# Quarter-size first loads, idle transposes, rstd from x^T and new planner figures in a transformer trunk kernel

## The chip, the cores and the metric

The kernel runs on one core of a Trainium2 chip. The metric is the device time of one execution in microseconds. Three runs of the kernel before gave 1015.75, 1016.25 and 1017.58 us; the median, 1016.25 us, is the time to beat. The engines are named as the profile names them: PE (TensorE matmul), PEld (its weight loads), DVE (VectorE), ACT (ScalarE), POOL (GpSimd) and SP, whose queue issues every DMA here.

## What is computed

A decoder trunk of two layers over 256 tokens of width 1024, all in float32. Each layer is FFN, mixer, FFN; layer 0 mixes by stick-breaking attention beside a convolution, layer 1 by gated linear attention (GLA). Every block is wrapped in norms:

```
def rms_norm(x, g):
    y = x * lax.rsqrt(jnp.mean(x * x, axis=-1, keepdims=True) + 1e-6)
    return y * g

h = x
for l in range(2):
    h = h + 0.5 * rms_norm(swiglu(rms_norm(h, g[0]), ffn1_in, ffn1_out), g[1])
    m = even_mixer(rms_norm(h, g[2])) if l == 0 else odd_mixer(rms_norm(h, g[2]))
    h = h + rms_norm(m, g[3])
    h = h + 0.5 * rms_norm(swiglu(rms_norm(h, g[4]), ffn2_in, ffn2_out), g[5])
```

Six phases follow each other, p = 0 to 5. The change rewrites the very start of phase 0: the norm of x that stands ahead of the first FFN.

## The kernel before

**Weights and products.** A weight block is 128x1024 float32, 512 KB. SP loads it into a ring of four `raw` buffers. ACT casts it to a rounded high part `hi` (L310), DVE subtracts that from the raw block to get the low part `lo` (L311), and both go into rings of nine. PE then makes each product three times, high by high, high by low and low by high (`mm3`, L334, L335, L336). So a block costs one DMA, one ACT cast, one DVE subtraction and a run of matmuls, and the buffers come free in that order.

**The planner.** The class `Plan` writes the order of every engine's instructions before the kernel is built. Each step is added with an estimated cost; a list scheduler then picks, among the steps that are ready, the one that comes first in the program. It adds `LATENCY` (80 ns) to each hand-over between engines, 1700 ns ahead of a DMA and 900 ns behind one, and takes a DMA to cost its bytes over 360. An engine keeps the order so written: whatever stands first on it and waits holds what stands behind it.

**The start (class `Entry`).** Phase 0 doesn't wait for the norm. The kernel also gets x transposed (`x_t`, two halves of 512 KB, L388) and the first gain (`g_first`, L390). ACT scales and rounds x^T by the gain (`xgh`, L395), DVE takes the rest (`xgl`, L397), and the first two groups of products `pt` (`proj_entry`, 48 matmuls of 512 columns each) run on these without rstd. Meanwhile x itself is loaded in four pieces (`h`, L300), ACT squares it with a running sum (L344), DVE adds epsilon (L349), and POOL raises the sum to the power -1/2 (`rstd_of`, L340). The gates of the first FFN (`ut`, L578 on ACT, L580 on DVE) apply rstd to the products. `scaled` then spreads rstd over a PSUM bank by two products (`rstd_rows`, L427), DVE multiplies x^T by it (L432, eight times), and ACT and DVE split that into `xT` (L442, L443), which all later products of this FFN (`pw`, L534 and L535) need.

**Later places that the prediction speaks of.** In each FFN the first four gates stand on PE banks that the later `pw` products take over: `pw` of the third pair waits until DVE has read the last gate `ut_11` (L584) from its bank. In GLA, PE makes the low-rank gate product `gz` (L937) from a small tile that DVE copies out of PSUM (`gla_small`, L932), amid the weight splits `lo_gq` (L311). The transposes of normed rows (`xtr_p`, L479) wait for DVE's `xn_p` (L467).

Of the kernel before, what the change touches and what calls it, by code (L numbers as in the profile page):

```python
# [9 lines left out]
F32 = mybir.dt.float32  # L10
# [26 lines left out]
OUT_TAIL = 8  # L37
CONV_PE = 6
# [29 lines left out]
class Plan:  # L68
# [3 lines left out]
    LATENCY = 80  # L72
    DMA_START, DMA_DONE = 1700, 900
# [60 lines left out]
    def dma(self, nbytes, fn, r, w):  # L134
        return self.add("dma", nbytes / 360.0, fn, r, w)
# [77 lines left out]
def trunk(ctx: ExitStack, tc: tile.TileContext, x, x_t, g_first, norm_g, ffn_in, ffn_out, hyb_in, hyb_out,  # L213
# [83 lines left out]
    def load_x(t):  # L297
        for n in range(2):
            s = slice(n * H, (n + 1) * H)
            dma(P * H * 4, lambda t=t, s=s: nc.sync.dma_start(h[t][:, s], x[t * P:(t + 1) * P, s]),  # L300
                [], [(h[t], n)])

    def load_gain(i):
        g = buf("gain", [P, D], F32, f"gain{i}")
        dma(P * D * 4, lambda: nc.sync.dma_start(g[:, :], norm_g[i].partition_broadcast(P)), [], [g])
# [7 lines left out]
    def weights(src, name, slots=None, first=False):  # L313

        res = []
        for i in range(src.shape[0]):
            raw = buf("raw", [P, D], F32, f"raw_{name}_{i}")
            dma(P * D * 4, lambda i=i, raw=raw: nc.sync.dma_start(raw[:, :], src[i]), [], [raw])
# [4 lines left out]
            if first and not i:  # L323
                for n in range(2):
                    s = slice(n * H, (n + 1) * H)
                    split(H, lambda hi=hi, s=s: hi[:, s], lambda lo=lo, s=s: lo[:, s], lambda raw=raw, s=s: raw[:, s], [raw], [(hi, n), (lo, n)])
# [12 lines left out]
    def rstd_of(st):  # L339
        gps(470, lambda: nc.gpsimd.tensor_tensor(st[:, 3:4], st[:, 2:3], mhalf[:, :], op=ALU.pow),  # L340
# [31 lines left out]
    class Entry:  # L372
# [14 lines left out]
        def load(self, b):  # L387
            dma(P * D * 4, lambda: nc.sync.dma_start(self.raw[b][:, :], x_t[b]), [], [self.raw[b]])  # L388
            if b == 0:
                dma(P * KT * 4, lambda: nc.sync.dma_start(self.gk[:, :], g_first), [], [self.gk])  # L390

        def split(self, b):
            raw, (hi, lo) = self.raw[b], (self.parts[q][b] for q in range(2))
            for k in range(4 * b, 4 * b + 4):
                act(S, lambda k=k: nc.scalar.activation(self.cols(hi, k), self.cols(raw, k), AF.Copy, scale=self.g(k)),  # L395
                    [raw, self.gk], [(hi, k)], ptrs=1)
                dve(S, lambda k=k: nc.vector.scalar_tensor_tensor(  # L397
                    self.cols(lo, k), self.cols(raw, k), self.g(k), self.cols(hi, k).bitcast(F32),
                    op0=ALU.mult, op1=ALU.subtract), [raw, self.gk, (hi, k)], [(lo, k)], ptr=True)
# [6 lines left out]

        def statistics(self):
            for t in range(NT):
                load_x(t)
            for t in range(NT):  # L410
                y, st = buf("y", [P, D], F32, f"xsq_p0{t}"), self.st[t]
                for n in range(2):
                    sum_squares(y, n * H, st, n, lambda t=t, n=n: h[t][:, n * H:(n + 1) * H], 1.0 / 32.0,
                                [(h[t], n)], False)
                add_eps(st, EPS)
                rstd_of(st)

        def scaled(self, xT):

            small = slot(6, "entry_small")  # L420
# [777 lines left out]
```

## Time and profile before

| what | us |
|---|---|
| median of three runs | 1016.25 |
| the profiled execution | 1020.89 |
| its span, first to last instruction | 1019.2 |
| PE busy in it | 1000.6 (98%) |
| DVE busy | 679.0 (67%) |
| ACT busy | 568.4 (56%) |
| DMA engines' mean share | about half |

The profiled execution is 4.64 us longer than the median; differences worked out from its trace are applied to the median. Times in rows are microseconds from the start of the span unless marked ns. A group of like instructions is shown in one row with a count, so the duration of such a row is that of the whole group. Matmul durations overlap: one that "took" 0.39 us may have the next behind it after 0.23 us, and spacing is then read from start to start.

### The profile page before, as it was taken

Reading aid. Unit: us, or ns where it says so; the run is one execution under the profiler, and the core shown is the slowest. Engines: PE = TensorE matmul, PEld = TensorE weight load, DVE = VectorE, ACT = ScalarE, POOL = GpSimd, SP = SyncE. Lnnn points to the kernel's source line nnn. Section 1 sums busy time; section 2 is a strip of 40 time slices with the busy share of each in tenths; the row PEclk is TensorE's granted clock in tenths of the full one; section 3 lists DMA queues with packets and bytes.
Section 4 is the critical chain, followed back from the end, with each engine's and each line's share of the span. In section 5 each row is a group of like instructions: output and inputs, shape, how many; then the busy total and the mean of one; then the engine's idle time right before and its main releaser. Section 6 shows DMA issues by size and latency. Waiting matters only on the chain.

```text
span 1019.2 us, 13982 instructions
## 1 busy us (share of the span) xinstructions
PE 1000.6 (98%) x5216; PEld 845.2 (83%) x5216; DVE 679.0 (67%) x1103; ACT 568.4 (56%) x979; POOL 57.2 (6%) x109
## 2 busy tenths in 40 slices
PE   6999999999999999999999999999999999999997
PEld 5888888888777888888888888888889888888885
DVE  4875658669868766668666666774568586656662
ACT  6764657585556654557455545654464375545551
POOL 2730000100001000000000000000000110000000
PEclk9999999999999999999999999999989999999999
DMA  8676557552034746567446465772641156555531
GB/s 320 220 251 200 180 195 257 197 174 76 21 125 165 266 162 213 166 207 237 162 171 211 161 215 164 231 246 84 211 166 64 42 182 231 182 190 187 199 110 42
DMA packets 50342, 180.46 MB, mean 177 GB/s; under 512 B 5713, under 2 KB 5969, under 8 KB 50274
## 3 DMA queue, kind: packets, MB, share of 16 engines
q1 hardware_dynamic: 50274, 179.57, 52.1%
q8 instruction: 41, 0.67, 0.3%
q14 instruction: 27, 0.22, 0.1%
HBM read 178.50 MB, written 1.05 MB: 176 GB/s over the span
## 4 chain that ended last, share of the span: by engine, by line
PE 92%; DVE 3%; DMA 2%; ACT 1%; issue 1%; POOL 1%; SPq 0%; DVEq 0%; POOLq 0%; ACTq 0%
PE pw L534 26%; PE pw L535 13%; PE o_f L334 8%; PE o_f L335 8%; PE o_f L336 8%; PE pt L335 2%; PE pt L334 2%; PE pt L336 2%; DMA raw_fi<-ffn_in 2%; PE gv L335 1%; PE gv L334 1%; PE gv L336 1%; PE cv L832 1%; PE sp L1027 1%; PE xtr_p L479 1%; PE hq L334 1%
## 5 line engine op out<-in xcount | busy, mean ns | idle before, releaser
L534 PE MATMUL pw<-xT_p,hi_fi 128*128 128x512 f32 x1152 | 409.8, 399 | 1.4 <-DVE ut L584 1.4
L535 PE MATMUL pw<-xT_p,lo_fi 128*128 128x256 f32 x1152 | 323.4, 281 | 0.0
L534 PEld LDWEIGHTS pw<-xT_p,hi_fi 128*128 128x128 f32 x1152 | 216.6, 188 | 55.4 <-issue 1.3
L311 DVE TENSOR_TENSOR lo_fi<-raw_fi,hi_fi 128x1024 fp32r<-128x1024 f32 (+1 forms) x177 | 212.7, 1216 | 50.8 <-ACT hi_fi L310 50.4
L535 PEld LDWEIGHTS pw<-xT_p,lo_fi 128*128 128x128 f32 x1152 | 217.8, 189 | 2.2
L310 ACT CAST hi_fi<-raw_fi 128x1024 fp32r<-128x1024 f32 (+1 forms) x177 | 181.2, 1045 | 42.7 <-DMA raw_fi<-ffn_in 22.7
L658 DVE TENSOR_TENSOR uab<-pw,uab 128x256 f32<-128x256 f32 x144 | 60.5, 421 | 114.3 <-ACT uab L657 114.3
L657 ACT COPY uab<-pw 128x256 f32<-128x256 f32 x144 | 53.6, 372 | 135.3 <-PE pw L535 135.0
L334 PE MATMUL o_f<-hi_fo,uTh 128*128 128x512 f32 x224 | 88.2, 394 | 0.0
L335 PE MATMUL o_f<-lo_fo,uTh 128*128 128x512 f32 x224 | 87.9, 392 | 0.0
L336 PE MATMUL o_f<-hi_fo,uTl 128*128 128x512 f32 x224 | 87.2, 389 | 0.0
L311 DVE TENSOR_TENSOR lo_fo<-raw_fo,hi_fo 128x1024 fp32r<-128x1024 f32 x56 | 68.3, 1222 | 13.4 <-ACT hi_fo L310 12.6
L310 ACT CAST hi_fo<-raw_fo 128x1024 fp32r<-128x1024 f32 x56 | 58.8, 1049 | 5.6 <-DMA raw_fo<-ffn_out 2.2
L340 POOL TENSOR_TENSOR pst_p<-pst_p,mhalf 128x1 f32<-128x1 f32 x12 | 8.2, 685 | 790.2 <-DVE pst_p L349 775.5
L334 PE MATMUL o_f<-h_fo,uTh 128*128 128x512 f32 x128 | 50.8, 397 | 0.0
L336 PE MATMUL o_f<-h_fo,uTl 128*128 128x512 f32 x128 | 50.5, 395 | 0.0
L335 PE MATMUL o_f<-l_fo,uTh 128*128 128x512 f32 x128 | 50.5, 394 | 0.0
L334 PEld LDWEIGHTS o_f<-hi_fo,uTh 128*128 128x128 f32 x224 | 42.1, 188 | 9.7
L336 PEld LDWEIGHTS o_f<-hi_fo,uTl 128*128 128x128 f32 x224 | 42.1, 188 | 9.2
L556 ACT CAST uTh<-uw 128x256 fp32r<-128x256 f32 x72 | 29.3, 407 | 35.7 <-DVE uw L660 35.5
L335 PEld LDWEIGHTS o_f<-lo_fo,uTh 128*128 128x128 f32 x224 | 42.1, 188 | 6.7
L659 ACT ACTIVATE uw<-uab 128x256 f32<-128x256 f32 x72 | 30.1, 418 | 31.1 <-DVE uab L658 31.1
(249 smaller groups left out, 1674.1 us busy)
## 6 DMA issues: line engine op xcount, KB each, us to landing
raw_fi<-ffn_in SPq DMA_DIRECT2D x176, 512.0 KB, 4.5
raw_fo<-ffn_out SPq DMA_DIRECT2D x88, 512.0 KB, 4.2
raw_gv<-gla_in SPq DMA_DIRECT2D x16, 512.0 KB, 4.5
gain<-norm_g SPq DMA_DIRECT2D x11, 512.0 KB, 4.6
raw_hu<-hyb_in SPq DMA_DIRECT2D x8, 512.0 KB, 4.7
raw_hq<-hyb_in SPq DMA_DIRECT2D x8, 512.0 KB, 4.1
raw_ho<-hyb_out SPq DMA_DIRECT2D x8, 512.0 KB, 4.3
raw_gq<-gla_in SPq DMA_DIRECT2D x8, 512.0 KB, 5.1
```

The source lines that it names most:

```text
L310: act(n, lambda: nc.scalar.copy(hi(), src()), r, [w[0]], psum=psum)
L311: dve(n, lambda: nc.vector.tensor_sub(lo(), src(), hi().bitcast(F32)), list(r) + [w[0]], [w[1]])
L334: nc.tensor.matmul(ps, lhsT=lhs[0], rhs=rhs[0], start=start, stop=False)
L335: nc.tensor.matmul(ps, lhsT=lhs[0], rhs=rhs[1], start=False, stop=False)
L336: nc.tensor.matmul(ps, lhsT=lhs[1], rhs=rhs[0], start=False, stop=stop)
L479: nc.tensor.transpose(ps[:, k * P:(k + 1) * P], y[:, c * P:(c + 1) * P], ident[:, :])
L534: nc.tensor.matmul(pss[i][:, :], lhsT=hi, rhs=xT[:, k, :, :], start=k == 0, stop=False)
L535: nc.tensor.matmul(pss[i][:, S:], lhsT=lo, rhs=xT[:, k, 0, :], start=False, stop=k == KT - 1)
L556: act(n, lambda: nc.scalar.copy(h_[:, s], src()), r, [(h_, 0), (h_, 1)], psum=psum)
L657: act(S, lambda v=v, ps=ps: nc.scalar.copy(v(), ps[:, S:]), [ps], [(g, i)], psum=True)
L658: dve(S, lambda v=v, ps=ps: nc.vector.tensor_add(v(), ps[:, :S], v()), [ps, (g, i)], [(g, i)])
L659: act(S, lambda u=u, g=g: nc.scalar.activation(u[:, :], g[:, :S], AF.Silu), [(g, 0)], [u], table=SILU)
```

## The change

Phase 0 begins in another way. PE first runs 24 transposes of the identity into a bank that nobody reads (`Entry.warm`). x^T comes in four loads of 256 KB, and the first weight block in two; the casts and scalings follow these pieces. The sum of squares is taken from x^T: ACT squares it without a running sum (two instructions of 128x1024), PE makes 16 products of a 128x128 block of squares by one column of ones (`entry_sums`, each product 128x1), DVE adds epsilon from that bank, POOL raises to the power as before. `scaled` comes ahead of the gates in the program. x itself and the first two gains, 2 MB in all, are loaded only halfway through the first FFN. The planner's figures change as well: `LATENCY` 150, 600 ns behind a DMA, bytes over 285, 690 ns for the power. These set the order of the whole program, so instructions move in all phases.

```diff
+WARM = 24
-    LATENCY = 80
-    DMA_START, DMA_DONE = 1700, 900
+    LATENCY = 150
+    DMA_START, DMA_DONE = 1700, 600
-    def dma(self, nbytes, fn, r, w):
-        return self.add("dma", nbytes / 360.0, fn, r, w)
+    def dma(self, nbytes, fn, r, w, after=()):
+        return self.add("dma", nbytes / 285.0, fn, r, w, after=after)
...
-        gps(470, lambda: nc.gpsimd.tensor_tensor(st[:, 3:4], st[:, 2:3], mhalf[:, :], op=ALU.pow),
+        gps(690, lambda: nc.gpsimd.tensor_tensor(st[:, 3:4], st[:, 2:3], mhalf[:, :], op=ALU.pow),
...
+        def load(self, i):
+            raw, s = self.raw[i // 2], slice(i % 2 * H, (i % 2 + 1) * H)
+            dma(P * H * 4, lambda: nc.sync.dma_start(raw[:, s], x_t[i // 2, :, s]), [], [(raw, 2 * i), (raw, 2 * i + 1)])
...
+        def warm(self):
+            ps = buf("out", [P, H], F32, "warm")
+            def run():
+                for _ in range(WARM):
+                    nc.tensor.transpose(ps[:, :P], ident[:, :], ident[:, :])
+            pe(WARM * 4 * P, run, [ident], [ps])
...
         def statistics(self):
+            small = self.small = slot(6, "entry_small")
+            fill((small, "1"), lambda: small[:, :P], 1.0)
+            sq = [buf("y", [P, D], F32, f"xsq_p0{b}") for b in range(2)]
+            for b in range(2):
+                act(D, lambda b=b: nc.scalar.activation(sq[b][:, :], self.raw[b][:, :], AF.Square, scale=1.0 / 32.0),
+                    [self.raw[b]], [sq[b]])
+            ps = bank("tr", "entry_sums")
+            def sums():
+                for t in range(NT):
+                    for k in range(KT):
+                        nc.tensor.matmul(ps[:, t:t + 1], lhsT=self.cols(sq[k // 4], k)[:, t * P:(t + 1) * P],
+                                         rhs=small[:, :1], start=k == 0, stop=k == KT - 1)
+            pe(2 * KT * 200, sums, [*sq, (small, "1")], [ps])
             for t in range(NT):
-                load_x(t)
...
+                dve(1, lambda t=t, st=st: nc.vector.tensor_scalar_add(st[:, 2:3], ps[:, t:t + 1], EPS), [ps], [st])
                 rstd_of(st)
...
+                        w = blocks(0, 1, True)
                         entry.load(1)
                         entry.split(1)
+                        w += blocks(1, 1)
+                        for i in (2, 3):
+                            entry.load(i)
+                            entry.split(i)
+                        entry.statistics()
...
+            if entry and j == NJ // 2:
+                entry.late = [plan.ops[-1]]
...
+                late = () if p else entry.late
+                if not p:
+                    for i in range(NT):
+                        load_x(i, late)
+                nxt["post"] = load_gain(layer * 6 + part * 2 + 1, late)
```

At the start ACT's order was this (`hi_fi_00_0` and `hi_fi_00_1` are the first two weight blocks, `x_t_180` and `x_t_209` the halves of x^T):

```order
L395 ACTIVATE xgh_195<-x_t_180,g_first 128x256 x4
L310 CAST hi_fi_00_0_206<-raw_fi_00_0_193 128x512 x2
L310 CAST hi_fi_00_1_219<-raw_fi_00_1_198 128x1024
L395 ACTIVATE xgh_232<-x_t_209,g_first 128x256 x4
L310 CAST hi_fi_01_0_249<-raw_fi_01_0_221 128x1024
L310 CAST hi_fi_01_1_262<-raw_fi_01_1_235 128x1024
```

It is now this (`hi_fi_t_0_226` and `hi_fi_t_0_248` are the first two weight blocks):

```order
L403 ACTIVATE xgh_220<-x_t_180,g_first 128x256 x2
L311 CAST hi_fi_t_0_226<-raw_fi_t_0_218 128x512 x2
L403 ACTIVATE xgh_220<-x_t_180,g_first 128x256 x2
L430 ACTIVATE xsq_p_239<-x_t_180 128x1024
L311 CAST hi_fi_t_0_248<-raw_fi_t_0_233 128x1024
L403 ACTIVATE xgh_258<-x_t_242,g_first 128x256 x4
L430 ACTIVATE xsq_p_276<-x_t_242 128x1024
L311 CAST hi_fi_t_0_285<-raw_fi_t_0_260 128x1024
L311 CAST hi_fi_t_1_311<-raw_fi_t_1_278 128x1024
```

The two squares now stand ahead of the casts of the second and of the third weight block. On PE, 18 matmuls of the first group of products stand between the transposes and the sums; the end of these and what follows reads now:

```order
L340 MATMUL pt_10_250<-hi_fi_t_0_248,xgh_220 128x512
L341 MATMUL pt_10_250<-lo_fi_t_0_262,xgh_220 128x512
L342 MATMUL pt_10_250<-hi_fi_t_0_248,xgl_224 128x512
L437 MATMUL entry_sums<-entry_small,xsq_p_239 128x1 x4
L437 MATMUL entry_sums<-entry_small,xsq_p_276 128x1 x4
```

The two rows of sums come once more for the second 128 tokens; the other 30 matmuls of the group stand behind them, and behind those the two `rstd_rows` products, where before they stood in the midst of the second group.

In the last FFN (and alike in the two before it) ACT's order around the last gate `ut_11` was this:

```order
L310 CAST hi_fi_6_0_8081<-raw_fi_6_0_8055 128x1024
L310 CAST hi_fi_6_1_8093<-raw_fi_6_1_8071 128x1024
L310 CAST uTh_0_7993<-ptr_10_8095 128x128
L583 ACTIVATE ut_11_8112<-pt_11_8041 128x256
L310 CAST hi_fo_2_0_8114<-raw_fo_2_0_8089 128x1024
```

It is now:

```order
L311 CAST hi_fi_6_0_8130<-raw_fi_6_0_8108 128x1024
L608 ACTIVATE ut_11_8139<-pt_11_8084 128x256
L311 CAST uTh_0_8034<-ptr_10_8132 128x128
L311 CAST hi_fi_6_1_8151<-raw_fi_6_1_8120 128x1024
L311 CAST uTh_1_8041<-ptr_10_8132 128x128
```

The gate and the small cast moved ahead of a weight cast that waits for a load; on DVE the second half of the gate moved ahead of that block's subtraction too.

In GLA, DVE's order around the copy of `gla_small` was this:

```order
L311 TENSOR_TENSOR lo_gq_0_6960<-raw_gq_0_6916,hi_gq_0_6932 128x1024
L918 TENSOR_TENSOR rg_6893<-rg_6893,gla_small 128x512
L311 TENSOR_TENSOR lo_gq_1_6969<-raw_gq_1_6928,hi_gq_1_6964 128x1024
L932 COPY gla_small<-glr 16x256
L311 TENSOR_TENSOR lo_gout_0_6991<-raw_gout_0_6962,hi_gout_0_6984 128x1024
```

It is now:

```order
L952 TENSOR_TENSOR rg_6936<-rg_6936,gla_small 128x512
L312 TENSOR_TENSOR lo_gq_0_7006<-raw_gq_0_6959,hi_gq_0_7001 128x1024
L966 COPY gla_small<-glr 16x256
L312 TENSOR_TENSOR lo_gq_1_7026<-raw_gq_1_6997,hi_gq_1_7008 128x1024
L312 TENSOR_TENSOR lo_gout_0_7038<-raw_gout_0_7004,hi_gout_0_7030 128x1024
```

The copy moved one weight split forward; PE's order there is the same: eight steps of `glr`, four of `gq`, then `gz`.

## Rows read from the trace of the kernel before

**Rows 1.** The page: busy time, share of the span, instructions of each engine.

```profile
PE 1000.6 (98%) x5216; PEld 845.2 (83%) x5216; DVE 679.0 (67%) x1103; ACT 568.4 (56%) x979; POOL 57.2 (6%) x109
```

**Rows 2.** PE's waits: line, releaser, us in total, times, longest.

```profile
PE pt L334 <- ACT hi_fi L310: 8.4, 1, 8.4
PE pw L534 <- DVE ut L584: 1.4, 2, 1.0
PE gz L937 <- DVE gla_small L932: 0.9, 1, 0.9
PE xtr_p L479 <- DVE xn_p L467: 0.5, 2, 0.3
```

**Rows 3.** The chain that ended last, its start: start, us, what.

```profile
1.73 5.98 DMA raw_fi<-ffn_in
7.73 0.63 ACT hi_fi L310
```

**Rows 4.** Windows: length, busy (instructions) of PE, PEld, DVE, ACT, POOL; clock, DMA, GB/s.

```profile
8.40:14.20 5.80, 5.80 (x13) 4.30 (x14) 5.37 (x9) 5.30 (x9) 0.00 (x0) 1.00 0.98 354
14.20:20.00 5.80, 5.80 (x26) 4.70 (x26) 3.60 (x4) 4.02 (x9) 0.51 (x1) 1.00 0.98 341
```

**Rows 5.** DMA issues, the one at 2.67 us: count, KB, us to landing.

```profile
x_t<-x_t SPq DMA_DIRECT2D x1, 512.0 KB, 7.6
```

**Rows 6.** ACT and DVE at the start: start, us, instruction [idle before].

```profile
4.67 1.70 ACT L395 ACTIVATE xgh<-x_t,g_first 128x256 fp32r<-128x256 f32 x4 [2.59 <-DMA g_first<-g_first]
...
16.84 1.05 ACT L310 CAST hi_fi<-raw_fi 128x1024 fp32r<-128x1024 f32 x1 [1.78 <-DMA raw_fi<-ffn_in]
17.79 0.63 ACT L344 ACTIVATE xsq_p<-h 128x512 f32<-128x512 f32 x1
...
24.54 3.22 DVE L432 SCALAR_TENSOR_TENSOR x_t<-x_t,g_first,rstd_rows 128x256 f32<-128x256 f32 x8 [0.79 <-PE rstd_rows L427]
```

**Rows 7.** PE from 21.2 us on: start, us, instruction [idle before].

```profile
22.27 0.39 PE L336 MATMUL pt<-hi_fi,xgl 128*128 128x512 f32 x1
...
23.89 0.61 PE L427 MATMUL rstd_rows<-entry_small 128*128 128x128 f32 x4
24.25 0.48 PE L334 MATMUL pt<-hi_fi,xgh 128*128 128x512 f32 x1
...
32.35 0.50 PE L335 MATMUL pt<-lo_fi,xgh 128*128 128x512 f32 x1 [0.21 <-DVE lo_fi L311]
...
35.02 0.39 PE L534 MATMUL pw<-xT_p,hi_fi 128*128 128x512 f32 x1
```

**Rows 8.** GLA, DVE and PE at 741 to 745 us, same columns.

```profile
741.65 1.22 DVE L311 TENSOR_TENSOR lo_gq<-raw_gq,hi_gq 128x1024 fp32r<-128x1024 f32 x1
...
742.10 0.28 PE L336 MATMUL gq<-xT_p,lo_gq 128*128 128x256 f32 x1
742.78 0.40 DVE L932 COPY gla_small<-glr 16x256 f32<-16x256 f32 x1
...
743.24 2.34 PE L937 MATMUL gz<-gla_small 17*128 17x512 f32 x4 [0.86 <-DVE gla_small L932]
```

**Rows 9.** Windows behind that place, and one of 40 us, columns as in rows 4.

```profile
744.00:746.00 2.00, 2.00 (x5) 0.67 (x4) 0.32 (x1) 1.58 (x2) 0.00 (x0) 0.68 0.96 383
746.00:748.00 2.00, 2.00 (x11) 2.00 (x11) 0.03 (x1) 1.99 (x5) 0.00 (x0) 0.50 0.82 287
...
750.00:752.00 2.00, 2.00 (x13) 2.00 (x13) 0.09 (x1) 1.17 (x2) 0.00 (x0) 0.61 0.00 0
...
757.00:797.00 40.00, 39.99 (x325) 38.77 (x324) 34.95 (x136) 20.20 (x49) 3.54 (x5) 1.00 0.23 78
```

**Rows 10.** The last FFN, ACT, DVE and PE at 849 to 853 us.

```profile
849.42 1.05 ACT L310 CAST hi_fi<-raw_fi 128x1024 fp32r<-128x1024 f32 x1 [0.74 <-DMA raw_fi<-ffn_in]
...
851.85 0.41 DVE L584 TENSOR_TENSOR ut<-ut,pt 128x256 f32<-128x256 f32 x1
...
852.40 0.47 PE L534 MATMUL pw<-xT_p,hi_fi 128*128 128x512 f32 x1 [0.97 <-DVE ut L584]
```

More of the change, by code (lines that the diff above doesn't have):

```diff
@@ L295, in trunk, with load_x @@
     h = [const(f"h{t}", [P, D]) for t in range(NT)]
-    def load_x(t):
+    def load_x(t, after):
         for n in range(2):
@@ L317, in weights @@
             raw = buf("raw", [P, D], F32, f"raw_{name}_{i}")
-            dma(P * D * 4, lambda i=i, raw=raw: nc.sync.dma_start(raw[:, :], src[i]), [], [raw])
+            if first and not i:
+                for n in range(2):
+                    s = slice(n * H, (n + 1) * H)
+                    dma(P * H * 4, lambda i=i, raw=raw, s=s: nc.sync.dma_start(raw[:, s], src[i, :, s]), [], [(raw, n)])
+            else:
+                dma(P * D * 4, lambda i=i, raw=raw: nc.sync.dma_start(raw[:, :], src[i]), [], [raw])
             if slots:
@@ L595, in gate, with blocks @@
             later.append(transposes)
-        def blocks(jp, h, first=False):
-            return weights(ffn_in[f][4 * jp + 2 * h:4 * jp + 2 * h + 2], f"fi{f}_{jp}{h}", first=first)
+        def blocks(i, n, first=False):
+            return weights(ffn_in[f][i:i + n], f"fi{f}_t{i}", first=first)
         ahead = []
@@ L604, in ffn @@
                 if t == 0:
-                    w = ahead.pop() if ahead else blocks(jp, 0, bool(entry))
-                    if entry and jp == 0:
+                    if ahead:
+                        wtok.append(ahead.pop())
+                    elif entry:
+                        w = blocks(0, 1, True)
                         entry.load(1)
                         entry.split(1)
-                    wtok.append(w + blocks(jp, 1))
+                        w += blocks(1, 1)
[3 more added lines that the diff above has]
+                        entry.statistics()
+                        wtok.append(w + blocks(2, 2))
+                    else:
+                        wtok.append(blocks(4 * jp, 4))
                     for i in range(2):
@@ L615, in ffn @@
                         if jp == 0:
-                            ahead.append(blocks(1, 0))
-                            entry.statistics()
+                            entry.scaled(xT)
+                            ahead.append(blocks(4, 4))
                         while later:
@@ L1106, in after @@
             if t == 0:
-                nxt["post"] = load_gain(layer * 6 + part * 2 + 1)
+                late = () if p else entry.late
[3 more added lines that the diff above has]
+                nxt["post"] = load_gain(layer * 6 + part * 2 + 1, late)
                 if p < phases - 1:
-                    nxt["gain"] = load_gain((p + 1) // 3 * 6 + (p + 1) % 3 * 2)
+                    nxt["gain"] = load_gain((p + 1) // 3 * 6 + (p + 1) % 3 * 2, late)
                     nxt["xT"] = new_xT(f"p{p + 1}")
```

38 lines of the change are left out of this document (14 added, 24 removed).

## The prediction

> **What bounds the kernel now.** I read the busy times first, then PE's list of waits, then the start step by step, then the places later in the program where PE waits. PE is busy 1000.6 us of 1019.2 [rows 1], so a change pays only where PE starts, waits or runs at a low clock. The list of waits names four that matter [rows 2]: 8.4 us for the first weights, 1.4 us in the FFNs for a bank, 0.9 us in GLA, 0.5 us for normed rows. The first is the largest and is the one that the change attacks. The profiled execution took 1020.89 us, 1.7 us more than its span and 4.64 more than the median of 1016.25; I work out differences on the span and take them from the median.
>
> **The start as it was.** The first block lands at 1.73 + 5.98 = 7.71 us, ACT's cast starts at 7.73 and takes 0.63 [rows 3], and PE starts at 8.40. The products there come 13 in 5.80 us, then 26 in 5.80 us [rows 4]: 0.45 us and then 0.223 us each for 512 columns, which is 1.2 and then 2.4 GHz (the clock column prints 1.00 in both, so the spacing has to be read). The last of the 48 products of the first group starts at 22.27; the second group ends where `pw` starts, at 35.02 [rows 7]. 35.02 is the mark by which I judge the whole start: `pw` needs `xT`, and from there on PE runs without waits.
>
> **Part 1, transposes and smaller loads.** Two landings give the rate. 1.03 MB (the first half of x^T and the first block) had landed by 7.71, and 2.1 MB (with the second block and the second half) by 2.67 + 7.6 = 10.27 [rows 3, 5]; so 256 KB come each 0.63 us. In the new order the first half block has 0.5 MB with it instead of 1.03 MB and lands some 1.3 to 2.4 us earlier (the larger if bytes flow slower in the first microseconds), at 5.3 to 6.4 us. With the cast of 0.63, PE starts at 6.0 to 7.1 instead of 8.4. The transposes need only the identity, and cost 24 times 0.11 us, the spacing of 128-column products (four of them took 0.36 us to the next start, which then took 0.09 longer than its like [rows 7]): 2.6 us, or 5.3 at the low clock, from 1.4 on. They end by 6.7 at the latest and lie under the wait for data. So PE gains up to 2.4 us at its start, and if the transposes bring the clock up, 13 products at 0.223 us less, 2.9 us.
>
> None of this is kept, because the next data is late. The second quarter pair of x^T lands about where the first block did, at 7.7 (1.03 MB), and from there ACT has no gap: two scalings at 0.40 each (four take 1.70 [rows 6], from start to start 0.40), the square of a 128x1024 half, the cast of the second block, four more scalings, the second square. The square is not in the trace in this size; a 128x512 square took 0.63 and a 128x1024 cast 1.05 (its 128x512 form 0.63 as well), so 1.05, or 0.93 from start to start when queued. That puts the cast of the second block at 9.5 to 10.5, DVE's low part 1.22 later (a 128x1024 subtraction [rows 8]) at 11.8, and the second square's end at 13.1. PE has only 12 products until then; they end at about 9.4, or 11.5 at the low clock. So products 13 to 18 run from 11.8 to 13.0 whatever the clock did before.
>
> **Part 2, the sums.** 16 products in full float32 are 32 passes, as the two `rstd_rows` products are four [rows 7]. Each pass has to load 128 columns of weights and stream one. The price isn't in the trace for one column; the nearest row is 0.11 us a pass, giving 3.5 us. From below, if the second pass shared its load, 1.8 us; from above, the low clock, 7.0 us. I take 3.5, since loading and not streaming sets the spacing of 128-column passes. They stand in PE's own order, so this is on the path: 13.1 to 16.6. The other 30 products take 6.96 us, and the first group ends at 23.5 instead of 22.27 + 0.23 = 22.50.
>
> Behind it the two `rstd_rows` (0.45), 48 products (11.14) and four transposes (0.45) give 35.5 for `pw`. Before, the same three sum to 12.04 of 12.52 us, so some 0.5 us of waiting, 0.2 of it named [rows 7], goes. The rest of the chain has room: DVE's eight multiplications (3.22 [rows 6]) and two subtractions of `xT` end near 31. **The start loses 0.5 us** with the clock up throughout; with sums at 1.8 us it would gain 1.2.
>
> **Part 3, the clock in the sums.** GLA shows what thin work does. PE stops after 742.10, waits 0.86 us and runs four passes of 17 rows [rows 8]; the clock column then reads 0.68, 0.50, 0.50 (the window left out of the rows is like the one ahead) and 0.61 over 8 us [rows 9], that is, 1.2 GHz for most of it. What it costs: 0.64 + 1.0 + 1.0 + 0.78 = 3.4 us of full clock, some 2.6 of them in products that now come each 0.21 us and not 0.12 (the windows hold 11 to 13 where 2 us hold some 17). In the new start PE has 1.4 us of wide products between 9.4 and 16.6 and else waits or runs one-column passes, which is thinner and longer than in GLA. I take it as likelier than not that the clock falls, late in the sums, for the price in GLA: 2.6 us.
>
> **Part 4, x and the gains later.** 2 MB (x and two gains) leave SP's queue ahead of 28 us and stand behind the weights of some 100 us. At the 354 GB/s of the start [rows 4] they take 5.7 us; the weight rings hold nine blocks, and PE's waits name no load but the first [rows 2]. I cost it at nothing; at worst one block is late by what of the 5.7 us the rings don't cover.
>
> **Part 5, the order.** In GLA, DVE copies `gla_small` one split earlier, so it ends 1.22 us sooner, at 742.78 + 0.40 - 1.22 = 741.96, ahead of the last `gq` product at 742.10 [rows 8]: the wait of 0.9 to 1.0 us goes. Without the stop, PE goes from wide products into 1.7 us of thin ones and out again, and the clock may hold: 2.6 to 3.4 more. In the three later FFNs a cast waits for a load until 849.42 and holds `ut_11` behind it, whose second half ends at 852.26, when `pw` starts, 0.97 idle [rows 10]. The gate now stands ahead of that cast and of its subtraction, so 1.4 us go [rows 2], to 1.9 with the slow restart. Two `xtr_p` groups stand six products later: 0.5 to 1.0. The sum is 0.9 + 2.6 + 1.4 + 0.5 = **5.4 us**, at most 7.3. What is late next is DVE, 34.95 of 40 us busy behind GLA with PE at 39.99 [rows 9]; at 87% it has room for 5.4, not much more, which is why I take the lower ends.
>
> **Sum.** -0.5 - 2.6 + 5.4 = 2.3 us faster: 1016.25 - 2.3 = **1013.9 us**.
>
> **The rivals.**
> - *The clock holds in the sums.* For it: the passes come without a gap, and a weight load each 0.11 us is no idle engine. Against: the fall in GLA followed less. Then 5.4 - 0.5 = 4.9 faster, 1011.4; with the upper ends 7.3 + 1.2, at the very best 1008.
> - *Slower: the clock isn't up before the sums or falls as they begin.* The sums then cost 7.0 and the 13 or so products behind them 0.223 each more, 2.9: together 6.4 more than in part 2, so 5.4 - 0.5 - 6.4 = 1.5 slower, 1017.8. It decides if at 13 us PE runs at 1.2 GHz. Before, the clock rose 5.8 us after the first product, with no gap between [rows 4]; the new start has 12 products, 5.4 us at the low clock, and then a wait. The transposes ahead of them are there to be counted too. The Trainium skill speaks against them: "TensorE: Matmul & The Clock Gate", Part 4, "PE-mode transpose", says that transposes do not count as PE work for the clock gate. By that rule the idle transposes change nothing and this rival's time holds; no row of this trace shows a stretch of transposes long enough to tell.
> - *The order gives little.* The clock falls in GLA all the same, since its 17-row passes remain, or DVE, pressed 5 us harder, makes PE wait elsewhere. Then of the 5.4 some 2.3 to 2.8 remain: 2.6 - 0.5 - 2.6 = 0.5 slower, 1016.7. For it: all planner figures changed, and an order can be worse in places that I did not follow.
> - *The change doesn't do what it says* for the start: PE begins earlier, but `pw` at 35.02 doesn't; that is in the forecast already.
>
> **How the numbers follow.** Forecast 0.42, clock holds 0.26, slower 0.17, order gives little 0.15. The range reaches from 1010.0, most of the second case, to 1018.3, most of the third. A measurement tells some 0.2% apart, 2.0 us: below 1014.2 is faster, above 1018.3 slower. The forecast lies about 0.24 below and 0.18 between; the second case 0.25 below; the third 0.07 between and 0.10 above; the fourth 0.01 below, 0.11 between, 0.03 above; with a little left for worse orders, faster 0.50, within 0.36, slower 0.14.
>
> **What would show it.** The first product at 6 to 7 us; a wait of PE near 10 to 11.8 for the second block; 32 passes of 0.11 us from about 13.1; `pw` first at 35 to 38, 38 if the clock falls; no wait at `gz` and a clock of 1.00 over 742 to 752, shifted; no `pw` wait on `ut`. I am wrong if the sums are far from 3.5 us, if the clock in the start goes another way, or if new waits stand in the list.

## The result, and the profile after

The changed kernel takes 1022.50 us (median of seven executions, 1020.34 to 1025.53) against 1015.84 (1015.09 to 1017.58): ratio 1.0065, 95% interval 1.0053 to 1.0078. It is 6.7 us slower where 2.3 us faster was forecast, and outside the range.

Of the page after, the line that answers to [rows 1]: PE is busy 5 us more, in a span of 1019.6 us.

```profile
PE 1005.4 (99%) x5272; PEld 851.2 (83%) x5272; DVE 680.8 (67%) x1103; ACT 568.8 (56%) x973; POOL 56.4 (6%) x109
```

PE's waits after (line, releaser, us in total, times, longest):

```profile
PE pt L341 <- DVE lo_fi_t L312: 1.5, 3, 0.8
...
PE xtr_p L504 <- DVE xn_p L492: 1.2, 1, 1.2
PE go L1083 <- DVE uTl_og L312: 1.2, 1, 1.2
PE pc L832 <- DVE e L827: 1.1, 2, 0.5
```

Of [rows 2] the 8.4 us for the first weights, the wait at `gz` and the one at `pw` are gone; `go` and `pc` are new, and `xtr_p` waits 0.7 us more.

PE's start after (start, us, instruction [idle before]), which answers to [rows 3, 7]:

```profile
1.43 4.64 PE L421 MATMUL warm<-ident 128*128 128x128 f32 x24 [1.43 <-POOL mhalf L257]
6.33 0.49 PE L340 MATMUL pt<-hi_fi_t,xgh 128*128 128x512 f32 x1 [0.25 <-ACT hi_fi_t L311]
...
9.49 0.39 PE L342 MATMUL pt<-hi_fi_t,xgl 128*128 128x512 f32 x1
10.26 0.49 PE L340 MATMUL pt<-hi_fi_t,xgh 128*128 128x512 f32 x1 [0.38 <-ACT hi_fi_t L311]
11.52 0.50 PE L341 MATMUL pt<-lo_fi_t,xgh 128*128 128x512 f32 x1 [0.77 <-DVE lo_fi_t L312]
...
12.78 4.42 PE L437 MATMUL entry_sums<-entry_small,xsq_p 128*128 128x1 f32 x32
17.05 0.77 PE L340 MATMUL pt<-hi_fi_t,xgh 128*128 128x512 f32 x1
17.62 0.63 PE L341 MATMUL pt<-lo_fi_t,xgh 128*128 128x512 f32 x1
...
22.29 0.40 PE L340 MATMUL pt<-hi_fi_t,xgh 128*128 128x512 f32 x1
...
38.49 0.48 PE L559 MATMUL pw<-xT_p,hi_fi 128*128 128x512 f32 x1
```

Windows of the same stretch (columns as in [rows 4]):

```profile
12.80:15.40 2.60, 2.60 (x26) 2.60 (x24) 1.47 (x2) 1.84 (x2) 0.00 (x0) 1.00 0.61 232
15.40:17.10 1.70, 1.70 (x10) 1.70 (x10) 0.00 (x0) 0.00 (x0) 0.00 (x0) 0.50 0.62 142
17.10:22.00 4.90, 4.90 (x13) 3.84 (x14) 2.95 (x5) 2.98 (x5) 4.31 (x5) 0.50 0.47 166
22.00:26.00 4.00, 4.00 (x18) 3.23 (x17) 2.03 (x2) 0.56 (x2) 3.73 (x10) 0.97 0.68 211
```

The new start is what was worked out, within some 0.3 us: first product at 6.33, a wait for the second block until 11.52, and the sums from 12.78 on. The passes come 0.11 us apart until 15.4 and 0.213 behind that. The granted clock falls 2.6 us into the sums and comes back at about 22, so that 12 wide products run 0.43 us apart. `pw` starts at 38.49 instead of 35.02.

GLA after, DVE and PE, answering to [rows 8], and two windows for [rows 9]:

```profile
746.19 0.40 DVE L966 COPY gla_small<-glr 16x256 f32<-16x256 f32 x1
...
747.20 0.28 PE L342 MATMUL gq<-xT_p,lo_gq 128*128 128x256 f32 x1
747.41 1.98 PE L971 MATMUL gz<-gla_small 17*128 17x512 f32 x4
```

```profile
747.00:749.00 2.00, 2.00 (x9) 0.94 (x7) 1.85 (x2) 0.96 (x2) 0.00 (x0) 1.00 0.78 258
749.00:751.00 2.00, 2.00 (x15) 1.69 (x15) 0.00 (x0) 1.72 (x3) 0.00 (x0) 1.00 0.81 301
```

The copy ends ahead of the last `gq` product, `gz` follows at once, and the clock holds. This too was forecast. From these two profiles alone the change would lose 0.4 us (1021.27 against 1020.89), while the medians lie 6.7 us apart. So the profile of before wasn't a usual execution of that kernel, and that is where the experiments begin.

### The profile page after: what moved, and what is told of

It is laid out like the page before. It is cut to its first block, busy times and chain, and to the rows that moved or that the text cites. A ratio compares the mean times of both kernels' runs of the same rounds, so it can differ in the third digit from the quotient of the medians.

```text
span 1019.6 us, 14083 instructions
## 1 busy us (share of the span) xinstructions
PE 1005.4 (99%) x5272; PEld 851.2 (83%) x5272; DVE 680.8 (67%) x1103; ACT 568.8 (56%) x973; POOL 56.4 (6%) x109
## 4 chain that ended last, share of the span: by engine, by line
PE 95%; DVE 2%; ACT 1%; DMA 1%; POOL 0%; issue 0%; SPq 0%; POOLq 0%; DVEq 0%; ACTq 0%
PE pw L559 26%; PE pw L560 13%; PE o_f L340 8%; PE o_f L341 8%; PE o_f L342 8%; PE pt L341 2%; PE pt L342 2%; PE pt L340 2%; PE sp L1061 1%; PE gv L342 1%; PE gv L341 1%; PE gv L340 1%; PE hq L340 1%; PE cv L866 1%; PE gq L340 1%; PE gq L342 1%
## 5 line engine op out<-in xcount | busy, mean ns | idle before, releaser
L312 DVE TENSOR_TENSOR lo_fi<-raw_fi,hi_fi 128x1024 fp32r<-128x1024 f32 x144 | 173.6, 1223 | 42.6 <-ACT hi_fi L311 42.2
L311 ACT CAST hi_fi<-raw_fi 128x1024 fp32r<-128x1024 f32 x144 | 148.3, 1050 | 27.8 <-PE o_f L342 18.8
```

Of the source, the lines that this page charges most:

```text
L311: act(n, lambda: nc.scalar.copy(hi(), src()), r, [w[0]], psum=psum)
L312: dve(n, lambda: nc.vector.tensor_sub(lo(), src(), hi().bitcast(F32)), list(r) + [w[0]], [w[1]])
```

## The experiments

In the tables "first pw" is where the first `pw` product starts, "gq to pe" the stretch of GLA from the first `gq` to the first `pe` product, "pw to end" the rest of the span behind the first pw, all in us from each kernel's one profile. Medians and ratios are of timed executions, each with the kernel before beside it on the same chip. That kernel's median is 1015.84 to 1016.60 us from chip to chip, so runs are best compared by their ratios.

| kernel | median | ratio to before, interval | first pw | gq to pe | pw to end |
|---|---|---|---|---|---|
| before, first profile | 1015.84 | | 35.02 | 16.11 | 984.1 |
| b_again | 1016.13 | 0.9998 (0.9986 to 1.0009) | 34.17 | 14.28 | 981.3 |
| changed | 1022.50 | 1.0065 (1.0053 to 1.0078) | 38.49 | 12.17 | 981.1 |
| a_oldfig | 1023.85 | 1.0069 (1.0052 to 1.0087) | 42.46 | 12.74 | 979.8 |
| b_newfig | 1016.94 | 1.0005 (0.9996 to 1.0014) | 35.41 | 12.17 | 981.0 |
| a_warm0 | 1020.56 | 1.0040 (1.0025 to 1.0055) | 36.93 | 12.17 | 981.0 |
| a_split | 1018.05 | 1.0017 (1.0003 to 1.0031) | 34.27 | 12.17 | 981.1 |
| a_sums48 | 1020.84 | 1.0035 (1.0023 to 1.0048) | 37.70 | 12.18 | 981.0 |
| a_oldstat | 1016.63 | 1.0002 (0.9990 to 1.0014) | 32.70 | 12.17 | 982.3 |
| b_warm | 1014.98 | 0.9984 (0.9972 to 0.9996) | 33.80 | 14.29 | 981.5 |
| b_glacopy | 1015.12 | 0.9988 (0.9977 to 0.9998) | 35.31 | 12.18 | 979.5 |
| c_oldstat | 1015.07 | 0.9985 (0.9974 to 0.9996) | 32.44 | 12.18 | 979.8 |
| c_split | 1018.88 | 1.0021 (1.0010 to 1.0033) | 41.61 | 12.17 | 980.3 |
| c_warm | 1015.14 | 0.9990 (0.9980 to 1.0000) | 34.51 | 12.17 | 979.2 |
| d_sums128 | 1018.32 | 1.0019 (1.0007 to 1.0032) | 35.34 | 12.17 | 981.1 |
| d_fill | 1020.78 | 1.0037 (1.0022 to 1.0052) | 38.66 | 12.17 | 981.0 |
| d_warm46 | 1019.93 | 1.0039 (1.0025 to 1.0054) | 33.64 | 12.18 | 988.3 |
| e_warm46 | 1016.01 | 0.9990 (0.9980 to 0.9999) | 33.42 | 12.18 | 983.9 |

### Which half loses: the start or the order

**b_again** is the kernel before, unchanged.

> The kernel before, unchanged, looked at once more. Its profiled execution took 1020.9 us against a median of 1016 us. Theory A (most executions of it lack the clock's fall in GLA, so the 3.4 us that I credited to the change were never in the median): a second profile of about 1016 us has a granted clock of 1.00 over 742 to 752 us, and gz follows gq with little wait. Theory B (the profiled execution is the usual one and the profile adds 4.6 us): the fall at 744.7 us is there again, and the profile again shows some 1020 us.

Its second profile took 1017.18 us. The clock still falls in GLA, but for a shorter time, as its windows show:

```profile
742.00:744.00 2.00, 2.00 (x5) 0.60 (x5) 0.96 (x1) 0.94 (x2) 0.00 (x0) 0.90 0.91 320
744.00:746.00 2.00, 2.00 (x10) 2.00 (x10) 0.00 (x0) 1.99 (x4) 0.00 (x0) 0.50 0.74 291
746.00:748.00 2.00, 2.00 (x15) 2.00 (x14) 0.69 (x1) 1.11 (x3) 0.00 (x0) 0.75 0.40 162
```

0.90, 0.50 and 0.75 make 1.7 us of full clock lost where [rows 9] made 3.4. The `pw` waits of 1.4 us [rows 2] are 0.2 us here. So neither theory is quite right: the fall is there in both profiles, but its length and the FFN waits differ from one execution to the next. The twelve executions take 1014.32 to 1019.33 us, with mean granted clocks from 0.998 or 0.999 (all those up to 1016.3) to 0.995 (the slowest). `b_newfig` and `b_glacopy` below, whose profiles show no fall ahead of the last 4 us of the span, have 0.998 or 0.999 in every execution. By that measure seven of these twelve had no fall in GLA either, and theory A holds for the usual execution. The first profile, 1020.89 at 0.994, lay beyond these twelve and beyond the 128 other executions of this kernel that were timed beside the later runs (at most 1020.85).

**a_oldfig** is the changed kernel with the old planner figures (those below, and 470 ns for the power), **b_newfig** the kernel before with the new ones:

```diff
-    LATENCY = 150
-    DMA_START, DMA_DONE = 1700, 600
+    LATENCY = 80
+    DMA_START, DMA_DONE = 1700, 900
...
-        return self.add("dma", nbytes / 285.0, fn, r, w, after=after)
+        return self.add("dma", nbytes / 360.0, fn, r, w, after=after)
```

> The changed kernel with the old planner figures (latency 80, 900 behind a DMA, bytes over 360, 470 for the power), so the new start alone. Theory A (the start loses 4.5 us by the sums and the clock's fall in them, the order gives little): pw first at 39 to 40 us, the fall in the sums as in the changed kernel, time 1019 to 1022. Theory C (the new order is what loses, through waits at go, xtr_p and pc that the kernel before did not have): 1016 to 1018.

> The kernel before with the new planner figures alone. Theory A: pw first at 35.0 as before, time 1014 to 1017. Theory C: 1019 or more, with the waits at go, xtr_p and pc in its list.

The start alone loses as much as the whole change (1.0069), the figures alone nothing that can be measured (1.0005). The new order has `b_newfig`'s waits:

```profile
PE xtr_p L479 <- DVE xn_p L467: 1.2, 1, 1.2
PE go L1049 <- DVE uTl_og L311: 1.2, 1, 1.2
PE pc L798 <- DVE e L793: 1.1, 2, 0.5
```

From the first pw to the start of the second FFN's `pw` it takes 309.6 us where `b_again` takes 307.4; from there to the end 671.4 against 673.9. It loses 2.2 us in and behind the attention and gains 2.5 behind that, 2.1 of it in GLA (14.28 to 12.17). The rival that blamed the order falls, but so does the gain that I gave it.

In `a_oldfig`'s profile the start is worse than in the changed kernel's:

```profile
9.14 0.40 PE L342 MATMUL pt<-hi_fi_t,xgl 128*128 128x512 f32 x1
11.08 0.50 PE L340 MATMUL pt<-hi_fi_t,xgh 128*128 128x512 f32 x1 [1.54 <-ACT hi_fi_t L311]
12.34 0.55 PE L341 MATMUL pt<-lo_fi_t,xgh 128*128 128x512 f32 x1 [0.76 <-DVE lo_fi_t L312]
...
14.40 6.82 PE L437 MATMUL entry_sums<-entry_small,xsq_p 128*128 128x1 f32 x32
```

```profile
12.60:14.40 1.80, 1.80 (x6) 1.35 (x6) 1.26 (x4) 1.80 (x3) 0.00 (x0) 0.52 0.81 259
```

Here the second quarter of x^T was first used at 8.23 and not at 7.00, since ACT waited 1.54 us for its load, which SP had issued at the same time (2.66 against 2.65). ACT's square and the cast of the second block came that much later, PE waited longer, the clock fell already at 12.7, ahead of the first one-column pass, and all 32 passes took 0.213 us: 6.82 us. This is the rival to which I gave 0.17, and it makes `pw` start at 42.46.

### What in the start loses

**a_warm0** sets `WARM = 0`.

```diff
-WARM = 24
+WARM = 0
```

> The changed kernel without the 24 transposes (WARM = 0), nothing else moved. Theory A (PE waits for the second block at 11.5 us whatever the clock did before): the first 12 products run 0.43 us apart and end near 11.6, the clock rises near 12, the sums begin near 13 and the clock falls in them all the same; time within 1 us of the changed kernel, 1021.5 to 1023.5. Theory D (the transposes earn their place): the clock is still low in the sums, which then take 6.8 us, and the time is 3 us or more above the changed kernel.

PE's start in it:

```profile
5.60 0.80 PE L340 MATMUL pt<-hi_fi_t,xgh 128*128 128x512 f32 x1 [5.60 <-ACT hi_fi_t L311]
...
9.06 0.53 PE L341 MATMUL pt<-lo_fi_t,xgh 128*128 128x512 f32 x1
9.43 0.39 PE L342 MATMUL pt<-hi_fi_t,xgl 128*128 128x512 f32 x1
...
12.82 3.76 PE L437 MATMUL entry_sums<-entry_small,xsq_p 128*128 128x1 f32 x32
...
17.02 0.63 PE L341 MATMUL pt<-lo_fi_t,xgh 128*128 128x512 f32 x1
```

The first products run at the low clock until 9.4 and it costs nothing, since PE waits for the second block until 11.57 in either case. The sums begin at the same time (12.82 against 12.78) and the passes now stay at 0.112 us to the end; the clock falls as they end (the product at 17.02 runs slow) and is back before 20. By the medians the kernel is some 2 us faster without the transposes, where I had put it within 1 us; the ratios are 1.0040 and 1.0065, with intervals that just touch. In the changed kernel the transposes are no gain.

**a_oldstat** takes the statistics from x again, loaded early. The rest stays, but for the loads of the next four weight blocks, which now stand two ahead of the statistics and two behind:

```diff
-            sq = [buf("y", [P, D], F32, f"xsq_p0{b}") for b in range(2)]
...
-            pe(2 * KT * 200, sums, [*sq, (small, "1")], [ps])
+            for t in range(NT):
+                load_x(t, ())
+            for t in range(NT):
+                y, st = buf("y", [P, D], F32, f"xsq_p0{t}"), self.st[t]
+                for n in range(2):
+                    sum_squares(y, n * H, st, n, lambda t=t, n=n: h[t][:, n * H:(n + 1) * H], 1.0 / 32.0,
+                                [(h[t], n)], False)
+                add_eps(st, EPS)
+                rstd_of(st)
```

> The changed kernel with the old statistics: x is loaded early in four pieces behind the first four weight blocks, squared by ACT with a running sum; no squares of x^T, no narrow products. The transposes, the 256 KB pieces, the late gains and the planner's figures stay. Theory A (the sums are what costs): no fall of the clock in the start, first group done by 20 to 21 us, pw at 32 to 33.5 us, the time 1013 to 1015.5. Theory G (the smaller loads or the transposes cost something themselves): pw at 35 or later, 1016 or more.

First pw at 32.70 and no fall: 5.8 us ahead of the changed kernel in the profile, 5.9 in the medians. Behind it, `pw` waits 1.0 us for a weight split that the order had put late, so the time came out 1 us above what was expected. The small pieces and the transposes as such cost nothing that can be measured (1.0002); the statistics from x^T, with x loaded late, do.

**a_split** and **a_sums48** move the sums. The first puts two or four products behind each step of six wide ones, the second all of them behind the 48.

```diff
+SUM_AT = (1, 2, 3, 3, 4, 5, 6, 7)
...
-            pe(2 * KT * 200, sums, [*sq, (small, "1")], [ps])
+                pe(400, run, [sq[k // 4], (small, "1")], pss, after=[plan.ops[-1]])
```

> The changed kernel with the 16 narrow products of the sums spread over the first group: two or four of them behind each step of six wide products, in two banks, nothing taken out. Theory A (the clock falls because the 32 thin passes stand in one piece behind a wait): no fall, the passes stay at 0.11 us, pw first at 34.5 to 36 us, the time 3 to 5 us below the changed kernel, 1017 to 1019. Theory E (the amount of thin work decides, wherever it stands): the clock falls as before and pw comes at 38 or later.

> The changed kernel with the sums in one piece, but behind all 48 wide products of the first group, so that no wait of PE stands ahead of them. Theory A1 (thin passes in one piece are enough): the clock falls some 2.6 us after they begin, pw at 37 to 39 us, the time near the changed kernel. Theory A2 (it needs the wait for the second block as well): no fall, pw at 34.5 to 36, the time 1017 to 1019.

Spread, the sums take nothing but their passes: 0.37 us for four, first pw at 34.27, no fall in the profile, 4.4 us off the median (1.0017 instead of 1.0065). PE in `a_sums48`:

```profile
20.63 3.63 PE L438 MATMUL entry_sums<-entry_small,xsq_p 128*128 128x1 f32 x32
24.11 0.68 PE L341 MATMUL pt<-hi_fi_t,xgh 128*128 128x512 f32 x1
```

In one piece behind the 48 products the sums begin at 20.63, and PE hasn't waited since 15.2. The clock falls as they end: the product at 24.11 runs slow, and pw comes at 37.70. That speaks for the passes as the cause. But `a_split`'s executions reach from 1016.91 us (clock 0.998) to 1022.41 (0.994), and the profile of **c_split**, the same sums with the old figures and one copy moved (below), shows a fall. It is that kernel's slowest execution (1023.59 us, the median being 1018.88):

> The changed kernel with the sums spread over the first group, the old planner figures, and the moved copy in GLA. Theory A: no fall of the clock in the start, pw first at 34 to 35.5, from there to the end 978 to 979.5, the time 1013 to 1016. If its runs spread over 5 us as those of the changed kernel with spread sums did (1016.9 to 1022.4), something other than the piece of thin passes still drops the clock in some executions.

```profile
10.35 0.58 PE L438 MATMUL entry_sums<-entry_small,xsq_p 128*128 128x1 f32 x4 [0.53 <-ACT xsq_p L431]
11.19 0.49 PE L341 MATMUL pt<-hi_fi_t,xgh 128*128 128x512 f32 x1 [0.27 <-ACT hi_fi_t L312]
12.45 0.79 PE L342 MATMUL pt<-lo_fi_t,xgh 128*128 128x512 f32 x1 [0.76 <-DVE lo_fi_t L313]
```

Between 9.7 and 12.45 PE ran four passes and one product there, and the product at 12.45 already runs slow. In `a_oldfig` the fall began with no one-column pass run at all. So the wait for the second block can go with a fall as well, and it was open which of the two does it in the changed kernel.

**d_sums128** keeps the wait and changes the passes (DVE then reads the first of the 128 columns); **d_fill** fills most of the wait and keeps the passes (not shown: `warm` gets a count, and the planner is told a cost of next to nothing):

```diff
-                        nc.tensor.matmul(ps[:, t:t + 1], lhsT=self.cols(sq[k // 4], k)[:, t * P:(t + 1) * P],
-                                         rhs=small[:, :1], start=k == 0, stop=k == KT - 1)
+                        nc.tensor.matmul(ps[:, t * P:(t + 1) * P], lhsT=self.cols(sq[k // 4], k)[:, t * P:(t + 1) * P],
+                                         rhs=small[:, :P], start=k == 0, stop=k == KT - 1)
```

```diff
+            if entry.spare and k == 1:
+                entry.warm(14, after=[plan.ops[-1]])
+                entry.spare = False
```

> The changed kernel with the sums against 128 columns of ones instead of one (128x128 products; every column holds the same sum, the first is used). As many passes, as many weight loads, at the same place. Theory A3 (the clock falls because each pass streams one column only): the passes stay 0.11 us apart, no fall in or behind them, pw first at 35 to 36.5 us, the time 1017.5 to 1019. Theory A4 (the wait ahead of them, or passes bound by loading as such): the clock falls at about 15.4 us all the same, pw at 38 or later, the time 1021 to 1024.

> The changed kernel with 14 more transposes behind the first 12 products, where PE waits from 9.7 to 11.5 us for the second block; the sums stay one column wide and in one piece. Theory A3 (the thin passes alone are enough): the fall comes as before, 2 to 3 us into the sums, pw at 38 to 39, the time within 1 us of the changed kernel. Theory A4 (the wait is what starts it): no fall, pw at 35 to 36.5, 1017.5 to 1019.

PE and two windows of `d_sums128`:

```profile
11.58 0.50 PE L341 MATMUL pt<-lo_fi_t,xgh 128*128 128x512 f32 x1 [0.76 <-DVE lo_fi_t L312]
...
12.85 3.73 PE L437 MATMUL entry_sums<-entry_small,xsq_p 128*128 128x128 f32 x32
```

```profile
12.80:16.50 3.70, 3.70 (x34) 3.66 (x34) 1.54 (x2) 1.91 (x3) 0.00 (x0) 1.00 0.63 197
16.50:20.00 3.50, 3.50 (x17) 2.84 (x16) 1.57 (x4) 1.58 (x4) 2.99 (x4) 1.00 0.60 218
```

The same for `d_fill`:

```profile
9.31 1.69 PE L421 MATMUL warm<-ident 128*128 128x128 f32 x14
...
11.73 0.50 PE L341 MATMUL pt<-lo_fi_t,xgh 128*128 128x512 f32 x1 [0.49 <-DVE lo_fi_t L312]
...
12.98 5.15 PE L437 MATMUL entry_sums<-entry_small,xsq_p 128*128 128x1 f32 x32
```

```profile
13.00:15.00 2.00, 2.00 (x19) 2.00 (x18) 1.32 (x2) 1.85 (x2) 0.00 (x0) 0.95 0.76 293
15.00:18.10 3.10, 3.10 (x16) 3.10 (x16) 0.16 (x1) 0.00 (x0) 0.00 (x0) 0.50 0.57 165
```

With 128 columns each pass costs what it cost with one, the wait ahead of it is the same (until 11.58), and the clock holds: in the profile, and by the mean clocks (0.997 to 0.999) in all twelve executions, which lie within 1017.57 to 1020.18 us. With one column, and PE's waits of 0.38 and 0.77 us cut to one of 0.49, the clock falls 2 us into the sums, and nine of ten executions stay at 0.994 to 0.996 and 1019.7 us or more. So in the changed kernel the fall goes when the passes get 128 columns, and doesn't go when most of the wait is filled. One number under `rhs` is worth 4 to 5 us (1.0065 to 1.0019).

The wait has its share all the same. `d_fill` isn't within 1 us of the changed kernel, as I had expected: 1.0037 against 1.0065, and the intervals don't touch. Against `d_sums128` the fall costs some 2 us in `d_fill`, and in `a_sums48` (1.0035) and `a_warm0` (1.0040) too, but nearly 5 in the changed kernel. That the rest comes of executions in which the clock falls ahead of the sums, as in `a_oldfig`'s profile, is likely but not shown.

### What would be faster

**b_glacopy** moves one copy of DVE in the kernel before, and `gz` with it:

```diff
-        dve(S, lambda: nc.vector.tensor_copy(lr()[:16, :], pl[:16, :S]), [pl, (ms, "lr")], [(ms, "lr")])
+        low = dve(S, lambda: nc.vector.tensor_copy(lr()[:16, :], pl[:16, :S]), [pl, (ms, "lr")], [(ms, "lr")])
+        low.prio, low.patience = low.prio - 400, 1000.0
```

> The kernel before with one step of DVE moved in GLA: the copy of gla_small goes ahead of the last two of its neighbours, and gz goes with it on PE; the planner's figures stay, and everything ahead of GLA stands as it stood. Theory A (that wait and the clock's fall behind it are the whole gain of the new order in GLA): no wait at gz, granted clock 1.00 over the 12 us behind it, the stretch from gq's first product to pe's first 12 to 12.5 us instead of 14.3 (16.1 in the first profile), the time 1013.5 to 1015 against 1016. Theory H (the clock falls from the thin passes alone): the stretch stays at 14 us or more and the time at 1015.5 or more.

From gq to pe 12.18 instead of 14.28, no fall, 0.12% faster: the GLA term alone, some 2 us in a profile and 1.2 in the medians. **b_warm** puts the 24 transposes ahead of the old start, **c_warm** does both, and **c_oldstat** is `a_oldstat` with the old figures and the moved copy.

```diff
     entry = Entry()
+    entry.warm()
     entry.load(0)
```

> The kernel before with the 24 transposes alone put ahead of everything on PE. Theory A (they count for the clock, and before's start, unlike the new one, is bound by PE's products from 8.4 to 22.5 us): products 0.23 us apart from the first on, the first group done by 20, pw at 32.5 to 34 us against 34.2 to 35.0, the time 1013.5 to 1015.5. By the rule that transposes do not count for the clock gate: the first 13 products 0.43 us apart as before, and the time 1016 to 1017.

> The kernel before with the 24 transposes ahead and the moved copy in GLA, nothing else. Theory A: pw first at 33 to 34, from there to the end 979 to 979.5, the time 1012.5 to 1014. Its profile of the transposes alone showed the clock low again from about 8 to 13 us, so if that is usual pw comes no earlier than 33.8.

> The start with transposes, 256 KB pieces and the old statistics, the old planner figures, and the moved copy in GLA. Theory A (the start gives 1.5 to 2.5 us, the moved copy 2, and the old figures spare the waits at pc and xtr_p in and behind attention, 2.3): pw first at 32 to 33.5, from there to the end 978 to 979.5, the time 1011 to 1013. Theory C' (what the new figures gain behind the attention isn't had with the old ones): from pw to the end 981 or more, the time 1014 or more.

`b_glacopy`, `b_warm`, `c_warm` and `c_oldstat` lie 0.1 to 0.16% below the kernel before (the interval of `c_warm` reaches 1.0000). `c_warm` and `c_oldstat` don't reach what the sum of their parts would give: the medians are 1015.14 and 1015.07 us, where I expected at most 1014 and 1013. `c_oldstat`'s profiled execution took 1013.98 us. `c_warm` shows why the transposes give little there:

```profile
1.43 5.20 PE L414 MATMUL warm<-ident 128*128 128x128 f32 x24 [1.43 <-POOL mhalf L257]
8.63 0.50 PE L335 MATMUL pt<-hi_fi,xgh 128*128 128x512 f32 x1 [2.00 <-ACT hi_fi L311]
...
10.09 0.63 PE L335 MATMUL pt<-hi_fi,xgh 128*128 128x512 f32 x1
```

They end at 6.6, PE has nothing until 8.63, and from 9.7 on (in `b_warm` from 9.3) the products run at the low clock after all. **d_warm46** makes the transposes last until the first block, `WARM = 46`; **e_warm46** does the same but tells the planner 24, so that the order is that of `c_warm`.

```diff
-WARM = 24
+WARM = 46
...
-            pe(WARM * 4 * P, run, [ident], [ps])
+            pe(24 * 4 * P, run, [ident], [ps])
```

The second of these edits is in `e_warm46` only.

> The kernel before with 46 transposes instead of 24 ahead, so that they last until about 8.2 us, when the first block is cast, and the moved copy in GLA. Theory A (in the version with 24 the clock fell at 9.7 us because PE had nothing from 6.2 to 8.6): products 0.23 us apart from the first on, pw first at 32 to 33.5, the time 1011.5 to 1013.5, 0.3 to 0.4% below the kernel before. Theory G (transposes hold the clock no better than idling): the fall near 10 as in that version, the time 1014 to 1016.

> The version with 24 transposes ahead of the old start and the moved copy in GLA, with 46 transposes instead, but told to the planner as 24, so that every other instruction stands where it stood there. Theory A (the 46 as such hold the clock until the first block; the loss in the run before came of the order, which put four weight splits of DVE ahead of a small one that pw waited 3.4 us for): no fall in the start, pw first at 32 to 33.5, no wait for uTl of over 0.5 us, the time 1011.5 to 1013.5. Theory I (46 transposes cost something themselves, whatever the order): 1016 or more.

`d_warm46`, PE's start and its longest wait:

```profile
8.27 0.48 PE L335 MATMUL pt<-hi_fi,xgh 128*128 128x512 f32 x1
...
19.78 0.39 PE L337 MATMUL pt<-hi_fi,xgl 128*128 128x512 f32 x1
```

```profile
PE pw L544 <- DVE uTl L312: 4.1, 2, 3.4
```

The clock holds and the first group is done at 20.0 instead of 22.5 us. But the planner, told of 46, had also moved weight splits of DVE ahead of the small `uTl`, for which `pw` then waited 3.4 us until 47.04; the clock fell in that wait, and the kernel is 0.39% slower than the kernel before. With the order kept, `e_warm46` starts `pw` at 33.42, 1.1 us ahead of `c_warm`; its median, 1016.01 over 1013.55 to 1019.05, doesn't tell it from `c_warm` (0.9990 both) and lies above the 1011.5 to 1013.5 that I expected. In its profile the clock rose only at 7.3, so the transposes held PE until 9.27, about 1 us after the first block's cast; and PE waited 2.0 us in the last FFN at the place of [rows 10]. What the 46 are worth in the median stays open.

## Why the prediction was wrong

**Part 1 held.** First product at 6.33 (6.0 to 7.1), the second block until 11.52 (11.8), and none of the earlier start kept.

**Part 2 was nearly right.** 32 passes at 0.11 us, as taken; without a fall they cost 3.7 us (`d_sums128`, and 3.76 in `a_warm0`), with one 4.4 to 6.8.

**Part 3, the clock: the right mechanism, mis-sized.** The fall came where it was put, "late in the sums", and I charged 2.6 us, the share of GLA's 3.4 that lay in the products behind. But the passes themselves are slowed as well: in the start from 0.112 to 0.213 us, and in GLA too, where `gz` took 2.34 us [rows 8] and takes 1.98 after. In the profile of the changed kernel the start lost 38.49 - 34.17 = 4.3 us against `b_again`, where 3.1 was forecast. In the median the start loses 6 to 7 us (1.0069 in `a_oldfig`; 1.0065 less the 1.0005 of the figures), and a start with the old statistics nothing (`a_oldstat`, 1.0002). What I missed is the spread: where a load came late, as in `a_oldfig`'s profile, the fall began ahead of the sums and lasted through all the passes. So the forecast and the "slower" rival were perhaps not two cases with one true, but two ends between which executions of one kernel lie. The times of the changed kernel, 1020.34 us at a mean clock of 0.996 to 1025.53 at 0.992, fit that; its one profile can't show it.

**Part 5, the order: the step that failed.** I took the 5.4 us as a sum of waits in one profile that would go. They did go: `gz`, the fall behind it and `pw` on `ut` are absent after. Two errors sat in the sum. First, I added rows of an execution 4.6 us above the median to a median that doesn't hold them. From the first pw to the end that execution took 984.1 us and `b_again` 981.3, so 2.8 of the 5.4 were no part of a usual execution. I had noted the 4.64 us and called it a difference to be carried over; it was a warning. Second, I followed the places where the new order takes a wait away and not those where it adds one. `pc`, `xtr_p` and `go` cost 2.2 us in and behind the attention (at `xtr_p` I had counted 0.5 gained, and it waits 0.7 more), which cancels the rest: pw to end 981.1 after, 981.3 in `b_again`, and 1.0005 for the figures alone. "An order can be worse in places that I did not follow" stood among the rivals at 0.15, and it is what happened. None of the four cases had it together with a fall dearer than 2.6, so the time lies outside them all.

**The sum, redone.** With the terms as measured: start 6 to 7 lost, order 0, so 1022 to 1023, where 1022.5 was measured. `d_sums128`, `d_fill` and `a_oldstat` divide the loss of the start. The fall costs 4 to 5 (1.0065 to 1.0019), of which 2 to 3 go when most of the wait is filled (1.0037). The passes, the squares and the late load of x cost some 1.7 (1.0019 to 1.0002, with intervals that overlap), the pieces, the transposes and the late gains nothing that can be measured.

**Rivals.** "The clock holds" is what `d_sums128` does, and it comes to 1018, not 1011.4, since the 5.4 wasn't there and the start without a fall costs more than the 0.5 that I gave it. "The change doesn't do what it says" came true for the transposes, in a way I hadn't written: they do raise the clock, and it isn't needed yet.

## What to carry to other kernels

Before waits of a profiled execution are summed into a gain, compare its time with the median: what it is longer by is in its rows, and a change can't take it out of the median. When a planner's figures change, follow the engines that wait after as closely as those that waited before, since here the new order paid for the waits it removed with others. The 32 passes of this kernel, during which PEld is busy throughout, cost no more with 128 columns than with one (3.73 and 3.76 us), and the clock held with 128. Where such passes stand in one piece, try giving them the columns (1.0019 here) or spreading them among wide products (1.0017, with a fall still likely in some executions).

## What the runs showed of the hardware

- **The clock rose under transposes.** In the changed kernel they come 0.213 us apart from 1.43 on, and from 5.25 on 0.109, with nothing else on PE; under the wide products of `a_warm0` it went the same way (0.43 us apart from 5.60, 0.23 from 9.43). It didn't always come so early: in `a_sums48` all 24 transposes come 0.213 us apart. The Trainium skill says in "TensorE: Matmul & The Clock Gate", Part 4, "PE-mode transpose", that transposes don't count as PE work for the clock gate; the trace of the changed kernel shows the clock rising under nothing but transposes, and the measurement decides. (The page's figures there are for bf16; these transposes are float32, and the profile lists them as MATMUL.)
- **It fell under one-column passes and stayed under 128-column ones.** 32 passes 0.112 us apart with one column had it fall 2.6 us on (changed kernel), 2 us on (`d_fill`) or as they ended (`a_sums48`, `a_warm0`); the same 32 with 128 columns, 0.112 us apart as well, did not (`d_sums128`). The profile shows PE 100% busy in both.
- **The fall isn't the same in each execution.** The changed kernel has mean clocks of 0.992 to 0.996 in its seven executions, the kernel before 0.994 to 0.999 in its own, and the times follow: 1025.53 us at 0.992, 1020.34 at 0.996. `b_newfig`, with no fall in its profile, keeps 0.999 in all twelve, within 1016.52 to 1018.16 us.
